# Another order of the weight places, activation sums in the plain units, and a closing step in one piece, in a two-block transformer kernel

## The chip, the core and the metric

The kernel runs on one NeuronCore of a Trainium2 chip. Times are device microseconds (us) of one execution of the whole program. Engines are named as the profile names them: PE does the matmuls, PEld loads their weights, DVE and ACT do the element-wise work, POOL does a little more of it, SP issues the DMAs. The kernel before takes 3473.58 us, the median of 3 runs (3473.26 to 3473.74).

## The reference, cut to what matters

Two transformer blocks over 512 tokens of width 1024, in float32. The first block is a modulated attention-like mixer with one feed-forward part; the second runs twice over: feed-forward, mixer, feed-forward, each followed by a layer norm. So there are five feed-forward parts, and the change lies in them:

```
def swiglu_2(x, w1, w2):
    g, u = jnp.split(x @ w1, 2, axis=-1)
    return (jax.nn.silu(g) * u) @ w2

for l in range(2):
    x = layer_norm(ALPHA * x + 0.5 * swiglu_2(x, ffn_w1[l, 0], ffn_w2[l, 0]), ...)
    x = layer_norm(ALPHA * x + hybrid_mixer_2(x, ...), ...)
    x = layer_norm(ALPHA * x + 0.5 * swiglu_2(x, ffn_w1[l, 1], ffn_w2[l, 1]), ...)
```

The hidden width is 2816, which is 11 column blocks of 256.

## The kernel before, in words

Every float32 operand of a matmul is held as two parts, a rounded value ("hi", cast by ACT) and the rest ("lo", a subtraction on DVE), and a product is three matmuls: hi by hi, hi by lo, lo by hi. In the trace `whi` and `wlo` are the parts of a weight, `xa` is the store of activations XA (its last two slots and some others also serve as weight places), `hl` is the same for the hidden activations, `pj` and `sd` are PSUM tiles.

A feed-forward part (function `ffn`) has three stages.

1. **Plain units.** The first 2 of the 11 hidden blocks are done by ordinary products (`unit`, `mm3`): half of the tokens (H0), then the other half (H1), the last unit whole. Weight pairs go round in a ring of six places: four pairs of slots of XA and two of their own; `plain_mode(e,i)` says at which the ring starts.
2. **Seven-product quads.** The other 9 hidden blocks, and most of the second matrix, are done as `Quad`s: a 2x2 block product with seven instead of eight products, which needs sums of activations (slots S1 to S4 of `Left`; `sums`, `sum4`) and sums of weights (`Quad.sum`). Function `run_quads` writes the order of PE, ACT, DVE and SP by hand, one slot per product: the products of the quads follow each other in a list `seq`; product 7 of a quad comes after product 1 of the next. In a slot come the product itself (`mm`), what closes the product before (`after`), weight sums (`sum`), left-over closing steps (`step`) and the casts of the weight two slots ahead (`cast`, `rest`). Three PSUM banks `sd` are kept: `after(1)` copies product 1 into a bank b (ACT L183), onto which product 2 then adds; product 2 can't start before that copy, and the copy not before the bank's last reader. `seven_mode` opens the stage with 12 small matmuls by zeros (L149), so that later matmuls may add to the banks.
3. **`stage2`**, the rest of the second matrix, and the layer norm.

The quads go in four groups. After each of groups 0, 1 and 2 stand two output quads (`out_quad`, o0 and o1), which read the hidden activations just made; they are called passages here, P1 (after one quad), P2 (after three) and P3 (after two). At a passage the last hidden quad still has to be closed: c12 adds and gates the first half (L258, L260), c21 gates the second (silu L265, L266), then sums for the next products (L110 to L113) and their split (L80 on ACT, L81 on DVE). An output quad adds its four quarters to X (L606, L607): its c22 reads E (a copy of product 4, `t` in the trace, or a bank) and bank b.

The activation sums of XA come in two parts (`e.sums(part,i)`, four tiles i each): part 0 is made in the plain units, part 1 by `extra` in the first slots of the quads; the sums of the two plain hidden blocks (`H.sums`) in slots 4 and 5. In the first feed-forward part (ffn1) all of XA's sums are made before `seven_mode`, and their operands are first remade from hi and lo (L1246). Outside `run_quads` a scheduler orders the instructions on each engine. On each engine all of them run in program order.

Of the kernel before, what the change touches and what calls it, by code (L numbers as in the profile page):

```python
# [88 lines left out]
class Left:  # L89
# [18 lines left out]
    def sum4(s,e,a,b):
        nc=e.nc; t=e.hs.tile([P,4,256],F32,tag="s",name="s",bufs=1)
        nc.vector.tensor_sub(t[:,1,:],b[:,0,:],b[:,1,:])  # L110
        nc.vector.tensor_sub(t[:,0,:],t[:,1,:],a[:,0,:])
        nc.vector.tensor_sub(t[:,2,:],a[:,0,:],b[:,0,:])
        nc.vector.tensor_add(t[:,3,:],t[:,0,:],a[:,1,:])  # L113
        return t
    def sums(s,e,i,a,b,part=None):

        nc=e.nc; n=4 if part is None else 2
        t=e.hs.tile([P,4,256],F32,tag="s",name="s",bufs=1)
        if part!=1:
            nc.vector.tensor_sub(t[:,1,:],b[:,0,:],b[:,1,:])  # L120
            nc.vector.tensor_sub(t[:,0,:],t[:,1,:],a[:,0,:])
        if part!=0: nc.vector.tensor_sub(t[:,n-2,:],a[:,0,:],b[:,0,:])
        if part is None: nc.vector.tensor_add(t[:,3,:],t[:,0,:],a[:,1,:])
        if part==1:
            nc.vector.tensor_sub(t[:,1,:],a[:,1,:],b[:,1,:])
            nc.vector.tensor_sub(t[:,1,:],t[:,1,:],t[:,0,:])
        s.put(e,s.S3 if part==1 else s.S2,n,i,t[:,:n,:])

# [67 lines left out]
def run_quads(e, quads, extra):  # L196
# [18 lines left out]
    with e.tc.manual_schedule(engines={ET.PE,ET.Activation,ET.DVE,ET.SP}):  # L215
        for s in range(min(at),len(seq)+1):
            for q,t in at.get(s,[]):
                if t in (0,5,6): q.load(e,t)
            put=None; keep=None
            if s>0: put=seq[s-1]  # L220
            if 0<=s<len(seq):
                q,j=seq[s]
                for d in q.needs:
                    if j==1: d.all(6)
                    if j==3: d.all(7)
                if j==2 and put==(q,1): q.after(e,1); put=None
                q.mm(e,j)
                if j==7 and s+1<len(seq) and seq[s+1][1]==2: keep=seq[s+1][0]
            if put and not (put[1]==1 and put[0] in done): put[0].after(e,put[1])
            for q,t in at.get(s,[]):  # L230
                if t in (1,2,3,4): q.sum(e,t)
            for q in quads:
                for j in (2,5,6,7):
                    if s>0 and (q,j)!=put: q.step(j)
            if keep in done: keep.after(e,1)
            for f in extra.get(s,[]): f()
            nx=seq[s+2] if 0<=s+2<len(seq) else None
            if nx: nx[0].cast(e,nx[1]); nx[0].rest(e,nx[1])
        for q in quads:
            for j in (2,5,6,7): q.all(j)  # L240
# [10 lines left out]

def gated(e, H, i, hscale, sums):

# [10 lines left out]
    def c21(ps):  # L264
        g=tmp(e); nc.scalar.activation(g,ps,AF.Silu)  # L265
        nc.vector.scalar_tensor_tensor(u.h[:,2:4,:],pair(g),hscale,pair(u.t),op0=ALU.mult,op1=ALU.mult)  # L266
    def c21b(ps):
        if sums: u.s=H.sum4(e,u.h[:,0:2,:],u.h[:,2:4,:])
        H.second(e,i,u.h[:,2:4,:])
    def c21c(ps):  # L270
        if sums: H.put(e,H.S2,4,i,u.s)
    u.c11,u.c12,u.c22,u.c21=[c11],[c12,c12b],[c22],[c21,c21b,c21c]
    return u

GAB=4
GROUPS=((0,3),(3,3),(6,2),(8,3))
PLAIN=2

def ffn(e, w1, w2, acc, hscale, ln):

    nc=e.nc
    with ExitStack() as cf:
# [116 lines left out]
class LN(Norm):  # L399
# [18 lines left out]
    def finish(s,sl):  # L418
# [13 lines left out]
        for i in range(4):  # L432
# [159 lines left out]
def second(e, D, out, layers=2):  # L592

    nc=e.nc
    for l in range(layers):
# [628 lines left out]
class RMS(Norm):  # L1224
# [4 lines left out]
    def finish(s,sl):  # L1229
# [150 lines left out]
```

## Time and profile before

| what | value |
|---|---|
| median of 3 runs | 3473.58 us |
| profiled execution, whole | 3473.03 us |
| its span in the trace | 3471.3 us |
| PE busy | 3272.6 us (94%) |
| DVE busy | 2538.6 us (73%) |
| ACT busy | 1701.5 us (49%) |
| granted TensorE clock, mean | 0.979 |

The stages in the trace (us from the span's start): block 1's mixer to 572, ffn1 from 612 to 1010, ffn2 from 1010 to 1385, a mixer, ffn3 from 1800 to 2235, ffn4 to 2570, a mixer, ffn5 from 3010 to the end. The stage of quads opens at 665, 1042, 1894, 2273 and 3126. The example in the text is mostly ffn3; the others have the same order.

### The profile page before, as it was taken

How to read it: one execution, taken by the hardware profiler on the slowest of the kernel's cores; microseconds unless marked ns; L12 is line 12 of the kernel's file. 1: busy time of each engine (PE TensorE's matmuls, PEld its weight loads, DVE VectorE, ACT ScalarE, POOL GpSimd, SP SyncE). 2: the span in 40 equal slices, each digit the busy share in tenths (PEclk: the TensorE clock that was granted, in tenths of full speed). 3: DMA queues.
4: the chain of work that ended last, by engine and by line, in shares of the span. 5: the costliest groups of instructions: out<-in, count | busy, mean ns of one | idle time of the engine just before them, and what ended most of it. 6: DMA issues, size and time to landing. Idle time of an engine off the chain costs nothing.

```text
span 3471.3 us, 54695 instructions
## 1 busy us (share of the span) xinstructions
PE 3272.6 (94%) x22056; PEld 2997.8 (86%) x22056; DVE 2538.6 (73%) x4061; ACT 1701.5 (49%) x2600; POOL 200.1 (6%) x237
## 2 busy tenths in 40 slices
PE   6979889999998999999999999989999999998998
PEld 3767779999998999878889999989998788898998
DVE  5858877798858988654456898778886634468987
ACT  4544534455544555762224555545556722244554
POOL 3241221000000000110000000000001100000000
PEclk9999999999999999999999999999999999999999
DMA  5221214222322233233331233322333233312231
GB/s 205 67 67 44 78 61 151 71 96 92 106 96 84 92 104 98 91 103 96 97 107 49 86 102 101 110 64 94 94 108 97 92 97 97 110 62 80 96 104 61
DMA packets 103502, 322.09 MB, mean 93 GB/s; under 512 B 11472, under 2 KB 15184, under 8 KB 103248
## 3 DMA queue, kind: packets, MB, share of 16 engines
q1 hardware_dynamic: 102464, 316.04, 28.2%
q8 instruction: 173, 2.83, 0.3%
q0 software_dynamic: 640, 2.10, 0.2%
q14 instruction: 81, 0.66, 0.1%
q10 hardware_dynamic: 144, 0.45, 0.0%
HBM read 316.45 MB, written 2.10 MB: 92 GB/s over the span
## 4 chain that ended last, share of the span: by engine, by line
PE 70%; DVE 16%; ACT 6%; issue 5%; POOL 1%; DMA 1%; ACTq 0%; SPq 0%; DVEq 0%; POOLq 0%
PE sd L134 15%; PE pj L134 12%; PE pj L70 7%; PE pj L71 6%; PE pj L72 6%; PE sd L70 6%; PE sd L71 6%; PE sd L72 6%; DVE wraw L167 2%; DVE wlo L172 1%; DVE cv L913 1%; ACT whi L170 1%; DVE xa L172 1%; DVE X L607 1%; DVE xa L44 1%
## 5 line engine op out<-in xcount | busy, mean ns | idle before, releaser
L43 ACT CAST xa<-wraw 128x1024 fp32r<-128x1024 f32 (+1 forms) x198 | 203.1, 1027 | 377.6 <-issue 172.9
L172 DVE TENSOR_TENSOR wlo<-wraw,whi 128x1024 fp32r<-128x1024 f32 (+2 forms) x310 | 333.5, 1076 | 57.8 <-ACT whi L170 54.0
L44 DVE TENSOR_TENSOR xa<-wraw,xa 128x1024 fp32r<-128x1024 f32 (+1 forms) x188 | 229.3, 1221 | 180.3 <-ACT xa L43 179.7
L70 PE MATMUL pj<-xa 128*128 128x512 f32 (+1 forms) x960 | 336.0, 352 | 3.3 <-ACT xa L80 1.7
L72 PE MATMUL pj<-xa 128*128 128x512 f32 (+1 forms) x960 | 336.3, 351 | 0.2 <-DVE xa L44 0.2
L71 PE MATMUL pj<-xa 128*128 128x512 f32 (+1 forms) x960 | 335.3, 350 | 0.1
L170 ACT CAST whi<-wraw 128x1024 fp32r<-128x1024 f32 (+2 forms) x310 | 286.4, 930 | 48.9 <-DVE wraw L167 24.4
L134 PE MATMUL sd<-xa,whi 128*128 128x256 f32 x2080 | 271.5, 283 | 1.9 <-ACT sd L185 1.9
L134 PEld LDWEIGHTS sd<-xa,whi 128*128 128x128 f32 x2080 | 259.6, 192 | 2.3 <-ACT sd L185 2.3
L70 PE MATMUL sd<-xa 128*128 128x512 f32 (+1 forms) x688 | 233.8, 342 | 2.7 <-ACT xa L80 1.7
L71 PE MATMUL sd<-xa 128*128 128x512 f32 (+1 forms) x688 | 234.8, 342 | 0.0
L72 PE MATMUL sd<-xa 128*128 128x512 f32 (+1 forms) x688 | 234.0, 341 | 0.0
L70 PEld LDWEIGHTS pj<-xa 128*128 128x128 f32 x960 | 184.5, 193 | 23.0 <-ACT X L957 2.0
L134 PE MATMUL pj<-xa,whi 128*128 128x256 f32 x1360 | 183.7, 289 | 20.4 <-ACT sd L183 20.3
L71 PEld LDWEIGHTS pj<-xa 128*128 128x128 f32 x960 | 185.0, 193 | 18.4 <-DVE xa L81 0.5
L72 PEld LDWEIGHTS pj<-xa 128*128 128x128 f32 x960 | 185.0, 193 | 18.0 <-DVE xa L44 0.4
L172 DVE TENSOR_TENSOR xa<-wraw,xa 128x1024 fp32r<-128x1024 f32 (+2 forms) x140 | 152.4, 1088 | 57.5 <-ACT xa L170 19.2
L134 PEld LDWEIGHTS pj<-xa,whi 128*128 128x128 f32 x1360 | 174.4, 198 | 22.7 <-ACT sd L183 22.7
L43 ACT CAST whi<-wraw 128x1024 fp32r<-128x1024 f32 (+1 forms) x90 | 89.4, 1001 | 180.5 <-PE pj L71 95.3
L134 PE MATMUL sd<-xa 128*128 128x256 f32 x1200 | 155.6, 287 | 8.7 <-ACT sd L187 8.7
L167 DVE TENSOR_TENSOR wraw<-wraw 128x1024 f32<-128x1024 f32 (+2 forms) x150 | 160.2, 1076 | 0.2 <-DMA wraw<-in_f_dram 0.2
L134 PEld LDWEIGHTS sd<-xa 128*128 128x128 f32 x1200 | 150.5, 196 | 9.8 <-ACT sd L187 9.8
(559 smaller groups left out, 8166.8 us busy)
## 6 DMA issues: line engine op xcount, KB each, us to landing
wraw<-in_f_dram SPq DMA_DIRECT2D x176, 512.0 KB, 4.1
wraw<-in_win_dram SPq DMA_DIRECT2D x144, 512.0 KB, 3.5
wraw<-in_f_dram SPq DMA_DIRECT2D x96, 384.0 KB, 3.2
wraw<-in_ff_dram SPq DMA_DIRECT2D x44, 512.0 KB, 4.0
raw<-in_ada_dram SPq DMA_DIRECT2D x48, 256.0 KB, 2.6
wraw<-in_ff_dram SPq DMA_DIRECT2D x24, 384.0 KB, 3.2
wraw<-in_ada_dram SPq DMA_DIRECT2D x16, 512.0 KB, 4.1
wraw<-in_f_dram SPq DMA_DIRECT2D x32, 256.0 KB, 2.8
```

The costliest lines, as they stand in the source:

```text
L43: nc.scalar.copy(hi[:,:n],raw[:,:n])
L44: (nc.gpsimd if e.wi%e.gp==0 else nc.vector).tensor_sub(lo[:,:n],raw[:,:n],hi[:,:n].bitcast(F32))
L70: nc.tensor.matmul(o,lhsT=hi[:,c],rhs=ah,start=start and k==k0,stop=False)
L71: nc.tensor.matmul(o,lhsT=hi[:,c],rhs=al,start=False,stop=False)
L72: nc.tensor.matmul(o,lhsT=lo[:,c],rhs=ah,start=False,stop=stop and k==nk-1)
L134: nc.tensor.matmul(ps[:,p*256:p*256+256],lhsT=w[:,j:j+128],rhs=A.t[:,c,k,l,:],start=first,stop=last,skip_group_check=True)
L167: n=s.n; e.nc.vector.tensor_add(o[:,:n],x[:,:n],y[:,:n])
L170: s.w[j]=hilo_tile(e); e.nc.scalar.copy(s.w[j][0][:,:s.n],s.raw(j)[:,:s.n])
L172: hi,lo=s.w[j]; n=s.n; e.nc.vector.tensor_sub(lo[:,:n],s.raw(j)[:,:n],hi[:,:n].bitcast(F32))
L607: else: nc.vector.tensor_tensor(x,x,ps,op=ALU.add if sgn>0 else ALU.subtract)
L913: nc.vector.scalar_tensor_tensor(a[:,o0:o0+n],ci[:,o0+i:o0+i+n],sc(i),a[:,o0:o0+n],op0=ALU.mult,op1=ALU.add)
```

## The change

Five edits:

- The weight ring starts at place 4 (before 0) in the plain units of a feed-forward part and of a mixer, at place 2 (before 4) in `stage2`, and at 1 (before 0) in the stage of quads.
- `seven_mode` clears each bank by one 128x512 matmul by zeros, in place of four 128x128 ones.
- All sums of XA, part 1 and then part 0, and the sums of the first plain hidden block, are made in the plain units (`hsums`, `e.sums`), in tiles of two instead of four; only those of the second plain hidden block are left in the quads, in slot 2.
- At the last hidden quad of a group all of c21 (gate, sums, their split) is issued in one piece (`at_once`). In slots where product 6 or 7 of that quad is closed, the weight sums and casts of the slot come before that closing (`late`).
- An output quad's c22 reads bank b first and then E.

The part on POOL gets no work that it didn't have: `v` is DVE everywhere.

```
     def sums(s,e,i,a,b,part,v=None,last=None):
         t=e.hs.tile([P,2,256],F32,tag="s",name="s",bufs=2)
...
+    def puts(s,e,i,part,t): s.put(e,s.S3 if part else s.S2,2,i,t)
...
-    e.fixed=[e.spare]; e.wide=False; e.wi=0
+    e.fixed=[e.spare]; e.wide=False; e.wi=1
     r=e.XA.t[:,0,0,:,:].rearrange("p l t -> p (l t)")
-    for t in e.sd:
-        for c in range(4): e.nc.tensor.matmul(t[:,c*128:c*128+128],lhsT=e.zero,rhs=e.zero,start=c==0,stop=True,skip_group_check=True)
+    for t in e.sd: e.nc.tensor.matmul(t,lhsT=e.zero,rhs=r,start=True,stop=True)
...
+            nx=seq[s+2] if 0<=s+2<len(seq) else None
+            late=put and put[1] in (6,7) and any(put[0] is q.needs[-1] for q in quads if q.needs)
+            def weights():
+                for q,t in at.get(s,[]):
+                    if t in (1,2,3,4): q.sum(e,t)
+                if nx and late: nx[0].cast(e,nx[1]); nx[0].rest(e,nx[1])
+            if late: weights()
             if put and not (put[1]==1 and put[0] in done): put[0].after(e,put[1])
-            for q,t in at.get(s,[]):
-                if t in (1,2,3,4): q.sum(e,t)
+            if not late: weights()
...
     def c21b(ps):
-        if sums: u.s=H.sum4(e,u.h[:,0:2,:],u.h[:,2:4,:])
+        if sums: u.p0=part(0); u.p1=part(1)
+        if last: H.puts(e,i,0,u.p0)
         H.second(e,i,u.h[:,2:4,:])
+        if last: H.puts(e,i,1,u.p1)
     def c21c(ps):
-        if sums: H.put(e,H.S2,4,i,u.s)
+        if sums and not last: H.puts(e,i,0,u.p0); H.puts(e,i,1,u.p1)
+    if last:
+        def at_once(ps): c21(ps); c21b(ps)
+        u.c21=[at_once]
...
-        plain_mode(e,0)
+        plain_mode(e,4)
...
+        def hsums(q):
+            a,b=hs[q][:,0:2,:],hs[q][:,2:4,:]; t=None
+            for p in (0,1): t=H.sums(e,q,a,b,p,None,t); H.puts(e,q,p,t)
...
-        for i in range(4): e.sums(0,i)
+        for q in range(PLAIN-1): hsums(q)
+        for p in (1,0):
+            for i in range(4): e.sums(p,i)
...
-                x={} if e.early else {0:[lambda: e.sums(1,0)],1:[lambda: e.sums(1,1)],2:[lambda: e.sums(1,2),lambda: e.sums(1,3)]}
-                for i,q in enumerate(range(PLAIN)): x[4+i]=[lambda q=q: H.sums(e,q,hs[q][:,0:2,:],hs[q][:,2:4,:])]
+                x={2: [lambda: hsums(PLAIN-1)]}
...
-    u.c22=[lambda ps,E: into(m+2,H1,E,1,True),lambda ps,E: into(m+2,H1,ps,-1,False)]
+    u.c22=[lambda ps,E: into(m+2,H1,ps,-1,True),lambda ps,E: into(m+2,H1,E,1,False)]
...
-    plain_mode(e,4)
+    plain_mode(e,2)
```

The line numbers shift; those used in the text are, before and after: prod's matmul L134 and L129, the zero matmul L149 and L143, copy of product 1 into b L183 and L177, cast of a weight L170 and L164, its rest L172 and L166, weight sums L167 and L161, c12 L258/L260 and L257/L259, c21 L265/L266 and L264/L265, sums L110 to L113 and L113/L114/L116/L120, sums of XA's part 1 L122/L125/L126 and L116/L118/L119, X L606/L607 and L615/L616.

**Where the quads of ffn3 open**, ACT, from the gate of the last plain unit (L294, after L300) to the first copy of a product 1 into its bank `sd_5190`. `xa<-s` is the cast of a sum of XA, `hl<-h` that of a hidden block. Before:

```order
L294 ACTIVATE t<-pj 128x512
L170 CAST xa<-wraw 128x1024
L170 CAST whi<-wraw 128x1024
L80 CAST hl<-h 128x2x256
L80 CAST hl<-h 128x256
L80 CAST xa<-s 128x2x256
L170 CAST whi<-wraw 128x1024
L183 COPY sd_5190<-pj 128x512
L80 CAST xa<-s 128x2x256
```

After:

```order
L300 ACTIVATE t<-pj 128x512
L80 CAST xa<-s 128x2x256 x2
L164 CAST whi<-wraw 128x1024
L164 CAST xa<-wraw 128x1024
L80 CAST hl<-h 128x2x256
L80 CAST hl<-h 128x256
L177 COPY sd_5190<-pj 128x512
```

The cast of a sum that stood between the hidden block and the copy is gone, and none follows the copy.

**Passage P2 of ffn3**, DVE, from the last quad's c22 (L263, after L262) to the last sum. `sd_5191` holds product 6 with what was added to it, `t_18874` and `t_18912` a weight sum, `hl<-h` and `hl<-s` are the rests of hidden activations and of their sums. Before:

```order
L263 TENSOR_TENSOR t<-t,sd_5190 128x512
L172 TENSOR_TENSOR xa<-wraw,xa 128x768
L258 TENSOR_TENSOR t<-sd_5191,t 128x512
L260 SCALAR_TENSOR_TENSOR h<-g_18804,t 128x512
L167 TENSOR_TENSOR wraw<-wraw 128x768
L172 TENSOR_TENSOR wlo<-wraw,whi 128x768
L81 TENSOR_TENSOR hl<-h,hl 128x2x256
L266 SCALAR_TENSOR_TENSOR h<-t 128x512
L167 TENSOR_TENSOR wraw<-wraw,t_18874 128x768
L172 TENSOR_TENSOR wlo<-wraw,whi 128x768
L110 TENSOR_TENSOR s<-h 128x256
L111 TENSOR_TENSOR s<-s,h 128x256
```

After:

```order
L262 TENSOR_TENSOR t<-t,sd_5190 128x512
L166 TENSOR_TENSOR wlo<-wraw,whi 128x768
L161 TENSOR_TENSOR wraw<-wraw 128x768
L166 TENSOR_TENSOR wlo<-wraw,whi 128x768
L257 TENSOR_TENSOR t<-sd_5191,t 128x512
L259 SCALAR_TENSOR_TENSOR h<-g_18837,t 128x512
L81 TENSOR_TENSOR hl<-h,hl 128x2x256
L161 TENSOR_TENSOR wraw<-wraw,t_18912 128x768
L166 TENSOR_TENSOR xa<-wraw,xa 128x768
L265 SCALAR_TENSOR_TENSOR h<-t 128x512
L113 TENSOR_TENSOR s<-h 128x256
L114 TENSOR_TENSOR s<-s,h 128x256
```

Two instructions on weights (L161, L166) now stand before L257 and L259 instead of behind. On ACT, in the same place, the copy of o0's product 1 (L177) stands behind the silu and the three casts of the piece (`hl<-s`, `hl<-h`, `hl<-s`); before, it stood behind the silu and one cast of a weight, ahead of `hl<-h` and `hl<-s`.

**The same passage, o0's quarters into X**, DVE; `sd_5190` is o0's bank b, which o1's copy of its product 1 takes next. Before:

```order
L607 TENSOR_TENSOR X<-X,t 128x2x256
L167 TENSOR_TENSOR wraw<-wraw,t_19073 128x768
L172 TENSOR_TENSOR wlo<-wraw,whi 128x768
L607 TENSOR_TENSOR X<-X,sd_5191 128x2x256
L607 TENSOR_TENSOR X<-X,sd_5190 128x2x256
```

After:

```order
L616 TENSOR_TENSOR X<-X,sd_5190 128x2x256
L161 TENSOR_TENSOR wraw<-wraw,t_19112 128x768
L166 TENSOR_TENSOR xa<-wraw,xa 128x768
L616 TENSOR_TENSOR X<-X,sd_5191 128x2x256
L616 TENSOR_TENSOR X<-X,t 128x2x256
```

The read of bank b moves ahead of two instructions on weights and of one on X, by one product of a quad.

## Rows read from the trace of the kernel before

**Rows 1.** The page: busy time, share of the span and instructions of each engine.

```profile
PE 3272.6 (94%) x22056; PEld 2997.8 (86%) x22056; DVE 2538.6 (73%) x4061; ACT 1701.5 (49%) x2600; POOL 200.1 (6%) x237
```

**Rows 2.** PE's waits: who waited for whom, us in total, times, longest.

```profile
PE pj L134 <- ACT sd L183: 45.1, 25, 3.6
PE pj L134 <- ACT hl L80: 10.8, 5, 2.2
PE sd L134 <- ACT sd L187: 8.7, 5, 2.2
PE pj L134 <- DVE hl L81: 6.8, 9, 1.3
PE pj L134 <- ACT whi L170: 5.5, 5, 1.7
...
PE sd L134 <- DVE hl L81: 4.4, 5, 0.9
...
PE pj L134 <- DVE xa L172: 3.0, 1, 3.0
...
PE sd L134 <- ACT sd L185: 1.9, 2, 1.7
...
PE sd L134 <- ACT hl L80: 1.7, 5, 0.3
```

**Rows 3.** Half-clock stretches (busy per engine, PEclk, DMA share, GB/s): one of 16, sum.

```profile
1928.23:1935.06 6.83, 5.02 (x22) 4.73 (x23) 6.79 (x12) 3.95 (x7) 0.00 (x0) 0.50 0.01 2
...
sum 71.66, PE 62.73 PEld 61.85 DVE 65.11 ACT 28.64 POOL 0.00; mean PE 3.92 PEld 3.87 DVE 4.07 ACT 1.79 POOL 0.00
```

**Rows 4.** Timeline where ffn3's quads open: start, length, engine, line, idle before.

```profile
1893.41 1.22 DVE L172 TENSOR_TENSOR xa<-wraw,xa 128x1024 fp32r<-128x1024 f32 x1 [9.37 <-PE pj L72]
...
1893.83 1.45 PE L149 MATMUL sd<-zero 128*128 128x128 f32 x12
...
1899.66 0.62 ACT L80 CAST xa<-s 128x512 fp32r<-128x512 f32 x1 [3.47 <-DVE s L126]
...
1901.13 0.58 ACT L183 COPY sd<-pj 128x512 f32<-128x512 f32 x1
...
1901.76 3.79 PE L134 MATMUL pj<-xa,whi 128*128 128x256 f32 x16 [3.56 <-ACT sd L183]
1902.40 0.42 DVE L122 TENSOR_TENSOR s<-X 128x256 f32<-128x256 f32 x1
1902.73 0.42 DVE L125 TENSOR_TENSOR s<-X 128x256 f32<-128x256 f32 x1
```

**Rows 5.** The waits on ACT: its copy into a bank, for the bank's reader.

```profile
ACT sd L183 <- DVE X L607: 69.2, 24, 4.1
```

**Rows 6.** Timeline of ffn3's passage P2, from c12 to o0's product 2.

```profile
2020.95 0.68 DVE L258 TENSOR_TENSOR t<-sd,t 128x512 f32<-128x512 f32 x1
2021.67 0.69 DVE L260 SCALAR_TENSOR_TENSOR h<-g,t 128x512 f32<-128x512 f32 x1
2022.28 0.95 DVE L167 TENSOR_TENSOR wraw<-wraw 128x768 f32<-128x768 f32 x1
...
2022.39 0.62 ACT L80 CAST hl<-h 128x512 fp32r<-128x512 f32 x1 [1.79 <-DVE h L260]
...
2023.36 1.24 PE L134 MATMUL pj<-hl,xa 128*128 128x256 f32 x9
...
2028.09 1.60 PE L134 MATMUL pj<-hl,whi 128*128 128x256 f32 x12
```

**Rows 7.** Timeline of ffn1 before its quads: remade operands on DVE, zeros on PE.

```profile
650.11 1.89 DVE L1246 TENSOR_TENSOR t<-xa 128x512 f32<-128x512 f32 x3
...
665.28 1.45 PE L149 MATMUL sd<-zero 128*128 128x128 f32 x12
```

**Rows 8.** PE alone in two stretches: the norm ffn3 to ffn4, block 1's last chain.

```profile
2222.23:2234.00 11.77, 11.15 (x88) 1.00 0.37 116
565.18:576.30 11.12, 10.72 (x90) 1.00 0.42 133
```

More of the change, by code (lines that the diff above doesn't have):

```diff
@@ L107, in second, with sums @@
         else: s.put(e,s.A22,1,i,b[:,1:2,:])
[L108 to L113, printed above, removed]
-        return t
[L115 to L127, printed above, removed]
+    def sums(s,e,i,a,b,part,v=None,last=None):
+        v=v or e.nc.vector
+        t=e.hs.tile([P,2,256],F32,tag="s",name="s",bufs=2)
+        if part==0:
+            v.tensor_sub(t[:,1,:],b[:,0,:],b[:,1,:])
+            v.tensor_sub(t[:,0,:],t[:,1,:],a[:,0,:])
+        else:
+            v.tensor_sub(t[:,0,:],a[:,0,:],b[:,0,:])
+            if last is None:
+                v.tensor_sub(t[:,1,:],a[:,1,:],b[:,1,:])
+                v.tensor_sub(t[:,1,:],t[:,1,:],t[:,0,:])
+            else: v.tensor_add(t[:,1,:],last[:,0,:],a[:,1,:])
+        return t
+    def puts(s,e,i,part,t): s.put(e,s.S3 if part else s.S2,2,i,t)
 def prod(e, ps, w, A, c, nk, start):
@@ L236, in run_quads @@
             for f in extra.get(s,[]): f()
-            nx=seq[s+2] if 0<=s+2<len(seq) else None
-            if nx: nx[0].cast(e,nx[1]); nx[0].rest(e,nx[1])
+            if nx and not late: nx[0].cast(e,nx[1]); nx[0].rest(e,nx[1])
         for q in quads:
@@ L250, in into_left, with gated @@
         if sums: H.sums(e,i,h[:,0:2,:],h[:,2:4,:])
-def gated(e, H, i, hscale, sums):
+def gated(e, H, i, hscale, sums, last):
     nc=e.nc; u=Use()
@@ L266, in c21, with part @@
         nc.vector.scalar_tensor_tensor(u.h[:,2:4,:],pair(g),hscale,pair(u.t),op0=ALU.mult,op1=ALU.mult)
+    v=nc.vector
+    def part(p): u.s=H.sums(e,i,u.h[:,0:2,:],u.h[:,2:4,:],p,v,p and u.s); return u.s
     def c21b(ps):
-        if sums: u.s=H.sum4(e,u.h[:,0:2,:],u.h[:,2:4,:])
+        if sums: u.p0=part(0); u.p1=part(1)
+        if last: H.puts(e,i,0,u.p0)
         H.second(e,i,u.h[:,2:4,:])
+        if last: H.puts(e,i,1,u.p1)
     def c21c(ps):
-        if sums: H.put(e,H.S2,4,i,u.s)
+        if sums and not last: H.puts(e,i,0,u.p0); H.puts(e,i,1,u.p1)
     u.c11,u.c12,u.c22,u.c21=[c11],[c12,c12b],[c22],[c21,c21b,c21c]
+    if last:
+        def at_once(ps): c21(ps); c21b(ps)
+        u.c21=[at_once]
     return u
@@ L306, in ffn @@
             for half in (0,1): into_left(e,H,j//2,hs[j//2],half,False)
-        if e.early:
-            for i in range(4): e.sums(1,i)
         seven_mode(e); Q=[]
@@ L311, in ffn @@
             last=g==len(GROUPS)-1
-            G=[Quad(e.XA,w1[j],4,gated(e,HP if last else H,j-j0,hscale,not last)) for j in range(max(j0,PLAIN),j0+n)]; Q+=G
+            G=[Quad(e.XA,w1[j],4,gated(e,HP if last else H,j-j0,hscale,not last,not last and j==j0+n-1)) for j in range(max(j0,PLAIN),j0+n)]; Q+=G
             if not last: Q+=[out_quad(e,H,w2[g][i],n,4*i,lambda m,sl,ps,sgn,new,g=g: acc(g,m,2,sl,pair(ps),sgn,new),() if i else G) for i in range(2)]
             else:
-                x={} if e.early else {0:[lambda: e.sums(1,0)],1:[lambda: e.sums(1,1)],2:[lambda: e.sums(1,2),lambda: e.sums(1,3)]}
-                for i,q in enumerate(range(PLAIN)): x[4+i]=[lambda q=q: H.sums(e,q,hs[q][:,0:2,:],hs[q][:,2:4,:])]
+                x={2: [lambda: hsums(PLAIN-1)]}
                 run_quads(e,Q,x)
@@ L439, in finish @@
             if s.out is None: s.to_left(sl,i,X[:,2*i:2*i+2,sl])
-        if sl is H1: e.sums=lambda part,i: e.XA.sums(e,i,X[:,2*i:2*i+2,H0],X[:,2*i:2*i+2,H1],part)
+        if sl is H1: e.sums=lambda part,i: e.XA.puts(e,i,part,e.XA.sums(e,i,X[:,2*i:2*i+2,H0],X[:,2*i:2*i+2,H1],part))
 def proj_units(units, first):
@@ L460, in mixer_in @@
 def mixer_in(e, mx, w_in, w_rg, w_oc, w_or, w_o, C, ln):
-    nc=e.nc; plain_mode(e,0)
+    nc=e.nc; plain_mode(e,4)
     uh=mx.tile([P,8,512],F32R,name="uh"); ul=mx.tile([P,8,512],F32R,name="ul"); U=Flat(uh,ul)
@@ L605, in acc @@
             x=e.X[:,m:m+2,sl] if n==2 else e.X[:,m,sl]
-            if g==0 and new: nc.vector.scalar_tensor_tensor(x,x,ALPHA,ps,op0=ALU.mult,op1=ALU.add)
-            else: nc.vector.tensor_tensor(x,x,ps,op=ALU.add if sgn>0 else ALU.subtract)
+            op=ALU.add if sgn>0 else ALU.subtract
+            if g==0 and new: nc.vector.scalar_tensor_tensor(x,x,ALPHA,ps,op0=ALU.mult,op1=op)
+            else: nc.vector.tensor_tensor(x,x,ps,op=op)
         def mk(i,o=None,r=1.0): return LN(e,C["ln_g"][:,8*i:8*i+8],C["ln_b"][:,8*i:8*i+8],1e-5,o,r)
@@ L1247, in sums @@
         def sums(part,i):
-            if s.b is None: e.XA.sums(e,i,X[:,2*i:2*i+2,H0],X[:,2*i:2*i+2,H1],part)
-            else: e.XA.sums(e,i,again(i,0),again(i,2),part)
-        if sl is H1: e.sums=sums; e.early=s.b is not None
+            a,b=[X[:,2*i:2*i+2,h] for h in (H0,H1)] if s.b is None else (again(i,0),again(i,2))
+            e.XA.puts(e,i,part,e.XA.sums(e,i,a,b,part))
+        if sl is H1: e.sums=sums
 def ada_piece(e,D,at,part,k,tag,raw):
```

## The prediction

> **What bounds the kernel now.** I read the page first, then PE's waits, the timeline around each kind of stop, and the granted clock by stretches. PE is busy for 94% of the span, DVE for 73% [rows 1]; so time can come only from PE's stops, from its clock, or from PE's work. PE's work hardly changes here. The stops that the quads of the five feed-forward parts make are nine lines of PE's waits: 45.1 + 10.8 + 8.7 + 6.8 + 5.5 + 4.4 + 3.0 + 1.9 + 1.7 = 87.9 us [rows 2]. And 16 stretches of 71.66 us in sum ran at half the clock (1.2 of 2.4 GHz), each at or behind a stop, which costs 71.66 / 2 = 35.8 us [rows 3]. More than about 124 us is not to be had.
>
> By place, the 87.9 us are of four kinds.
> - *Opening.* In ffn3 product 2 waits 3.56 us for the copy of product 1 into its bank; the copy stands on ACT behind the cast of a sum of XA, which had ACT idle for 3.47 us before it, for DVE [rows 4]. In all five parts this is 14.6 of the 45.1 us, and the 3.0 and 1.9 us: 19.5.
> - *Product 7 of the first quad*, behind the hidden sums in slots 4 and 5: the 8.7 us, one stop in each part.
> - *Passages.* P1 has 10.8 + 5.5 and five of the nine waits of the 6.8; P3 has the 4.4 and 1.7. Together 29.2 us with the 0.8 of P2, nearly all in P1.
> - *Bank b of an output quad.* Five stops in each part but one: o1's product 2 at P1, P2, P3 and the next quad's product 2 wait for a copy that itself waits for the last reader of the bank, L607 [rows 5]. That is 45.1 − 14.6 = 30.5 us.
>
> **The change, part by part.**
>
> *Sums of XA and of the first hidden block in the plain units.* In ffn2 to ffn5 nothing but the two casts of the hidden block stands ahead of the first copy on ACT. Left is the bare exchange of product 1, copy, product 2: the copy took 0.58 us and product 2 followed 0.63 us after its start [rows 4]; with PE's end ahead of it I take 0.95 us, between 0.63 and the 3.56 of before. Four times: 3.8 us. The sums must fit on DVE: one of part 1 is three subtractions at a step of 0.34 us, the dependent one 0.45, and a rest of about 0.6: 1.75 us, four times 7.0; the hidden sums are four and two rests, 2.8. Those 9.8 us stand against a hole of 9.37 us ahead of DVE's last weight rest before the quads [rows 4]; the first quad's own weight rest comes before the last four sums on DVE in these parts, so I count no stop. In ffn1 it comes behind all of them, and there the operands are remade first: from 650.1 us on DVE has 16 such additions at 0.6 us (1.89 for three, [rows 7]), 9.7 us, sums of 4 x (1.4 + 1.75) = 12.6, hidden ones 2.8, and some 4 of gates and rests: to 679 us. PE wants that rest at 665.28 + 0.7 + 16 x 0.12 = 668 [rows 7]: a stop of 11, with the copy 11.6 us. Its bounds are the 5.1 of before (nothing gets later) and 15. Opening: 3.8 + 11.6 = 15.4, from 19.5.
>
> *Only one set of hidden sums, in slot 2.* Its casts stand two slots ahead of the copy that product 7 waits for. 8.7 goes to 0; what is late next is the copy itself, 0.6 us in each part at the most.
>
> *c22 reads bank b first.* The bank comes free one product earlier, 1.45 to 2.9 us; the stops at o1 were at most 3.6 and mostly 0.8 to 2 long. I leave 0.3 in each part, 1.5 from 30.5. Hidden by PE's product; if DVE is a whole product late, 10 us come back.
>
> *The piece at passages.* At P1 the hidden sums that blocked ACT are gone, and o0's product 1 finds its data. But the copy that o0's product 2 waits for stands behind the whole piece on ACT, with only two products 1 to cover it. At P2, DVE has two weight instructions more ahead of L257, each 0.95 us long and 0.87 from start to start: L257 moves from 2020.95 to 2022.7, h is ready 0.72 + 0.69 later, its cast (0.62) ends at 2024.75, against PE's 2023.36 [rows 6]: a stop of 1.4. Then the products 1 of o0 and o1 last 2 x 2.2 us, to 2029.2. Meanwhile DVE has 0.6 (rest), 2 x 0.87 (weights), 0.6 (gate) and four sums of about 0.4, to 2029.3, ACT's casts follow with about 1.2, then the copy's 0.63: 2031.0. That stop is 1.8; P2 costs 3.2, from 0.16. At P3 the weights are narrower, but so are the covering products: 3.2 again. At P1 only the second stop remains, 1.75. Sum 8.15, in five parts 40.8, from 29.2. Bounds: the bare exchange of 0.95 at each passage (14) and P1 as it was, (10.8 + 5.5 + 6.8) / 5 = 4.6 [rows 2], at each (69). I take the worked-out value.
>
> *Zeros.* Twelve matmuls of 128 columns take 1.45 us [rows 4]; three of 512 take 3 x 0.23 if 256 columns take 0.12, as the quads' do (9 in 1.24, [rows 6]). 5 x 0.75 = 3.8 saved, at least 0, since twelve to three can't be slower.
>
> *The ring's start and the order outside the quads.* These shift what the scheduler lays under the norms. Between ffn3 and ffn4, 88 PE instructions lay under the norm's chain, 63 of them matmuls of the next units [rows 8]; now about 17: 46 x 0.12 = 5.6 us lost. In block 1's last chain about 60 of 90 [rows 8] are gone from under it; all of them would be 7.2, some of it is cover that wasn't needed; I take 4. These 9.6 have bounds of 0 and 13.
>
> *Clock.* Stops that stay are followed by half clock as the rows had it: each P2 and P3 one stretch of 3.4 us (10 x 1.7 = 17 lost), ffn1's opening 6.8 (3.4), the norm and the end 4.5: 25, from 35.8. Bounds: 8 (no passage is followed) and 51 (every passage by 6.83 us, as P1 of ffn3 was, [rows 3]).
>
> A stop as P2's, in two parts of under 2 us, is the open case. P1 of ffn3 had three, of 2.2 us at the most [rows 2], and 6.83 us at half clock [rows 3]. The Trainium skill (TensorE: Matmul & The Clock Gate, section "HAM oscillation — how this bites in real kernels") says that one long idle gap between bursts makes the next burst start throttled; by that alone P2 and P3 would be free of it, 17 us less, and the result 3421. Its next section ("A second HAM failure mode: psum-queue depth-cycling") says that frequent short stops at the turn of PSUM banks do it as well; this one the trace bears out, and it speaks against the piece.
>
> *Sum.* Stops: 15.4 + 0 + 1.5 + 40.8 = 57.7, from 87.9: −30.2. Zeros −3.8, cover +9.6, clock −10.8. Together −35.2: 3473.03 − 35.2 = 3437.8 for a profiled execution; the median of the runs shown lies 0.55 above it: 3438.
>
> **The rivals.**
> - *The passages are free.* If DVE is done earlier than I lay it (it was 73% busy overall), only the exchange is left: 40.8 falls to 14 and the clock's loss to 8. −27 − 17: 3394. For it: every waiting instruction moved was moved ahead of need. Against: the copy stands behind three casts, whatever DVE does.
> - *The passages cost as much as P1 did.* 15 x 4.6 = 69 in place of 40.8, and 9 more of clock: 3438 + 28 + 9 = 3475, no change. For it: P1's stops came from the very work that is now in one piece at all three. Against: it had double sums there.
> - *Slower: DVE is behind when the quads open.* The 9.8 us of sums go into a hole of 9.37, and they also wait for the XA slots that the weights leave, which the new ring decides. If in ffn2 to ffn5 the first weight rest is late as in ffn1, each has 10 us more of stop and 3.4 of clock: 4 x 13.4 = 54, 3492. It decides from 9 us a part on. Against: the rest stands ahead of the last sums.
>
> **How the numbers follow.** The forecast has 0.62, with its own range 3420 to 3456 (clock −17 or +9, passages ±10); free passages 0.14, dear passages 0.11, DVE behind 0.13. No change is within 0.2%, 7 us. Faster by more has 0.62 + 0.14 + 0.02 = 0.78, slower by more 0.11 + 0.03 = 0.14, the rest 0.08. The range goes from 3402 to 3478: it leaves out half of the free passages, most of DVE behind and a part of the dear ones.
>
> **What would show it.** Right: PE's wait for the copy into b at one place per passage (15 times, 1.7 to 2.4 us) and nearly none at o1; no wait for product 7's copy; one stop of 10 us or more in ffn1's opening and about 1 us in the others; ffn3 to ffn4 longer by 5 us; half clock near 50 us in the feed-forward parts. Wrong: stops of 5 us at the openings of ffn2 to ffn5 (the third rival), waits at P2 and P3 over 4 us or under 1 us.

## The result, and the profile after

The changed kernel takes 3426.51 us, the median of 4 runs (3419.30 to 3430.60), against 3473.42 before (4 runs): a ratio of 0.9861, interval 0.9846 to 0.9876. It is faster by 47 us; 35 were forecast, and the time lies inside the range given. The profiled execution is the longest of the four, 3430.60 us (3473.03 before).

The page's first part after, to set beside [rows 1]:

```profile
PE 3263.1 (95%) x22011; PEld 2989.2 (87%) x22011; DVE 2539.7 (74%) x4101; ACT 1709.2 (50%) x2640; POOL 199.3 (6%) x237
```

The work is the same but for 45 zero matmuls fewer. PE's idle time in the span fell from 3471.3 − 3272.6 = 198.7 us to 3428.8 − 3263.1 = 165.7, its busy time by 9.5: stops and clock have moved. PE's waits after, those of the quads (who waited for whom, us in total, times, longest), answer to [rows 2]:

```profile
PE pj L129 <- ACT sd L177: 33.1, 22, 2.2
...
PE pj L129 <- DVE wlo L166: 8.8, 5, 6.0
...
PE pj L129 <- DVE hl L81: 5.1, 15, 0.3
...
PE pj L129 <- ACT hl L80: 3.2, 10, 1.0
...
PE sd L143 <- ACT t L300: 2.7, 1, 2.7
...
PE pj L129 <- DVE xa L166: 0.5, 1, 0.5
```

They come to 53.4 us, from 87.9. The wait for product 7's copy (8.7) is gone. The copy L177 is waited for 22 times: at five openings, at 15 passages before o0's product 2 (1.7 to 2.2 us each), and twice in ffn3 for a bank b (0.90 before o1's product 2 at P3, 0.82 before the next quad's). DVE's reads of X no longer hold that copy: [rows 5] with its 69.2 us has no counterpart among ACT's longest waits. Of the waits for L166 only the 6.0 belongs to ffn1's opening. The other four (1.14 in ffn1, 0.57 or 0.58 in ffn2, ffn4 and ffn5) and the 0.5 are new: they stand in and behind P3, four of them in the product 2 that waited for bank b before. There the rest of a weight on DVE now comes last.

P2 of ffn3, the timeline after (start, length, engine, line, idle before), answers to [rows 6]:

```profile
1999.20 0.68 DVE L257 TENSOR_TENSOR t<-sd,t 128x512 f32<-128x512 f32 x1
...
1999.92 0.69 DVE L259 SCALAR_TENSOR_TENSOR h<-g,t 128x512 f32<-128x512 f32 x1
1999.96 1.12 PE L129 MATMUL pj<-hl,whi 128*128 128x256 f32 x8
2000.64 0.62 ACT L80 CAST hl<-h 128x512 fp32r<-128x512 f32 x1 [3.44 <-DVE h L259]
...
2001.32 0.38 PE L129 MATMUL pj<-hl,whi 128*128 128x256 f32 x1 [0.23 <-ACT hl L80]
...
2002.04 0.61 PE L129 MATMUL pj<-hl,whi 128*128 128x256 f32 x3 [0.34 <-DVE hl L81]
...
2005.28 0.62 ACT L80 CAST hl<-s 128x512 fp32r<-128x512 f32 x1 [2.79 <-DVE s L114]
...
2006.11 0.62 ACT L80 CAST hl<-s 128x512 fp32r<-128x512 f32 x1
...
2006.63 0.58 ACT L177 COPY sd<-pj 128x512 f32<-128x512 f32 x1
...
2007.26 3.92 PE L129 MATMUL pj<-hl,xa 128*128 128x256 f32 x18 [1.73 <-ACT sd L177]
```

Read it from below: o0's product 2 starts 0.63 us after the start of its copy, which ran behind the casts of the piece, the first of which had ACT idle for 2.79 us, for DVE's sums. All five P2 look like this (in ffn4 the first stop is 0.98 in place of 0.23), P1 too.

ffn1's opening after, PE alone:

```profile
673.83 0.62 PE L143 MATMUL sd<-xa,zero 128*128 128x512 f32 x2
...
679.04 0.49 PE L143 MATMUL sd<-xa,zero 128*128 128x512 f32 x1 [2.67 <-ACT t L300]
...
685.51 2.08 PE L129 MATMUL pj<-xa,wlo 128*128 128x256 f32 x8 [5.98 <-DVE wlo L166]
...
688.34 2.08 PE L129 MATMUL pj<-xa,whi 128*128 128x256 f32 x8 [0.74 <-ACT sd L177]
```

9.4 us, where it was 5.1. The stretches at half clock in ffn1 to ffn5 (columns as in [rows 3]), the first, one at a passage, the one in the norm behind ffn3, and the sum of 8:

```profile
679.63:693.28 13.65, 7.02 (x31) 6.73 (x32) 11.38 (x18) 4.66 (x7) 0.00 (x0) 0.50 0.09 29
...
2007.41:2010.82 3.41, 3.41 (x17) 3.41 (x18) 1.98 (x3) 1.94 (x3) 0.00 (x0) 0.50 0.00 0
...
2205.38:2215.62 10.24, 9.66 (x43) 9.39 (x44) 5.88 (x11) 3.44 (x6) 0.00 (x0) 0.50 0.49 148
...
sum 44.35, PE 37.14 PEld 36.58 DVE 30.29 ACT 15.91 POOL 0.00; mean PE 4.64 PEld 4.57 DVE 3.79 ACT 1.99 POOL 0.00
```

44.35 us against 71.66, so 13.7 us regained, if half of a stretch's length counts as lost. And two losses outside the quads, PE in the stretch from the norm's first matmuls by `ident` (L364, after L372) behind ffn3 to ffn4's first product, and from 500 us to ffn1's first product, after:

```profile
2192.75:2259.52 66.77, 62.60 (x438) 0.92 0.18 58
499.96:674.29 174.33, 165.78 (x1183) 0.97 0.34 110
```

and before:

```profile
2213.35:2274.23 60.88, 59.59 (x447) 1.00 0.26 89
495.30:666.57 171.27, 165.51 (x1194) 0.98 0.35 112
```

5.9 and 3.1 us lost. The 10.24 us at half clock of the norm lie inside the first stretch, so 5.1 of its 5.9 us stand in the 44.35 already, and 0.8 is left. Between the two executions 4.7 us more were also spent before 500 us, where the order of PE did not change, and 3 us less in the second mixer, where two half-clock stretches are missing. The 4.7 us are the spread of executions: PE's 2400th matmul starts between 483.8 and 490.2 us in the 14 kernels traced here, and latest in this trace.

### The profile page after: what moved, and what is told of

Same layout as the page of the kernel before. It is cut to its first block, busy times and chain, and to the rows that moved or that the text cites. A ratio compares the mean times of both kernels' runs of the same rounds, so it can differ in the third digit from the quotient of the medians.

```text
span 3428.8 us, 54643 instructions
## 1 busy us (share of the span) xinstructions
PE 3263.1 (95%) x22011; PEld 2989.2 (87%) x22011; DVE 2539.7 (74%) x4101; ACT 1709.2 (50%) x2640; POOL 199.3 (6%) x237
## 5 line engine op out<-in xcount | busy, mean ns | idle before, releaser
L166 DVE TENSOR_TENSOR wlo<-wraw,whi 128x1024 fp32r<-128x1024 f32 (+2 forms) x295 | 316.3, 1074 | 48.3 <-ACT whi L164 46.1
L70 PE MATMUL pj<-xa 128*128 128x512 f32 (+1 forms) x968 | 343.1, 355 | 1.4 <-ACT X L966 1.4
L72 PE MATMUL pj<-xa 128*128 128x512 f32 (+1 forms) x968 | 341.9, 354 | 0.0
L71 PE MATMUL pj<-xa 128*128 128x512 f32 (+1 forms) x968 | 341.3, 353 | 0.0
L164 ACT CAST whi<-wraw 128x1024 fp32r<-128x1024 f32 (+2 forms) x295 | 272.3, 926 | 61.5 <-DVE wraw L161 26.2
L129 PE MATMUL sd<-xa,whi 128*128 128x256 f32 x1760 | 229.1, 283 | 0.0
L129 PEld LDWEIGHTS sd<-xa,whi 128*128 128x128 f32 x1760 | 219.1, 192 | 0.0
L129 PE MATMUL sd<-xa 128*128 128x256 f32 x1680 | 213.0, 283 | 0.0
L129 PEld LDWEIGHTS sd<-xa 128*128 128x128 f32 x1680 | 206.6, 192 | 0.0
L71 PE MATMUL sd<-xa 128*128 128x512 f32 (+1 forms) x600 | 204.7, 341 | 0.0
L70 PE MATMUL sd<-xa 128*128 128x512 f32 (+1 forms) x600 | 203.8, 341 | 0.9 <-DVE X L1230 0.9
L129 PE MATMUL pj<-xa,whi 128*128 128x256 f32 x1520 | 200.0, 285 | 4.2 <-ACT sd L177 4.2
L72 PE MATMUL sd<-xa 128*128 128x512 f32 (+1 forms) x600 | 203.8, 340 | 0.0
L129 PEld LDWEIGHTS pj<-xa,whi 128*128 128x128 f32 x1520 | 190.9, 193 | 5.9 <-ACT sd L177 5.5
L44 DVE TENSOR_TENSOR wlo<-wraw,whi 128x1024 fp32r<-128x1024 f32 (+1 forms) x88 | 109.1, 1241 | 97.6 <-ACT whi L43 97.1
L166 DVE TENSOR_TENSOR xa<-wraw,xa 128x1024 fp32r<-128x1024 f32 (+2 forms) x155 | 169.5, 1094 | 16.0 <-ACT xa L164 14.4
```

Of the source, the lines that this page charges most:

```text
L44: (nc.gpsimd if e.wi%e.gp==0 else nc.vector).tensor_sub(lo[:,:n],raw[:,:n],hi[:,:n].bitcast(F32))
L70: nc.tensor.matmul(o,lhsT=hi[:,c],rhs=ah,start=start and k==k0,stop=False)
L71: nc.tensor.matmul(o,lhsT=hi[:,c],rhs=al,start=False,stop=False)
L72: nc.tensor.matmul(o,lhsT=lo[:,c],rhs=ah,start=False,stop=stop and k==nk-1)
L129: nc.tensor.matmul(ps[:,p*256:p*256+256],lhsT=w[:,j:j+128],rhs=A.t[:,c,k,l,:],start=first,stop=last,skip_group_check=True)
L164: s.w[j]=hilo_tile(e); e.nc.scalar.copy(s.w[j][0][:,:s.n],s.raw(j)[:,:s.n])
```

## The experiments

All were run beside the kernel before on the same chip; medians in us, with their runs. Experiments on the changed kernel are read against its 3426.5 (3419.3 to 3430.6). It was not run again beside them; the kernel before had medians of 3471.3 to 3474.4 there, so differences of less than about 3 us mean nothing.

**The bank read undone** (on the changed kernel):

```
-    u.c22=[lambda ps,E: into(m+2,H1,ps,-1,True),lambda ps,E: into(m+2,H1,E,1,False)]
+    u.c22=[lambda ps,E: into(m+2,H1,E,1,True),lambda ps,E: into(m+2,H1,ps,-1,False)]
```

> The changed kernel with one thing undone: the output quads' c22 reads E first and bank b second, as before. Theory (the bank that comes free a product earlier was the largest single saving): the stops at o1's product 2 and at the next quad's product 2 come back, about 30 us of PE waiting for the copy L177 at these places, and 3 to 9 us of half clock behind them: 3455 to 3466 us. Rival (o1 was relieved because the sums left the slots around it, c22's order is worth little): 3424 to 3432 us, and no new stop at o1.

3464.6 (3457.1 to 3469.4): 38 us lost by one swapped line. PE's waits:

```profile
PE pj L129 <- ACT sd L177: 65.1, 40, 4.4
```

18 more waits for the copy than the changed kernel has, 32 us more, as the theory had it. Against that the small waits for L166 are gone; only ffn1's 6.0 is left:

```profile
PE pj L129 <- DVE wlo L166: 6.0, 1, 6.0
```

ffn3's worst, before o1's product 2 at P3, shows the chain whole:

```profile
2106.09 1.28 DVE L616 TENSOR_TENSOR X<-X,sd 128x512 f32<-128x512 f32 x2
...
2107.45 0.57 ACT L177 COPY sd<-pj 128x512 f32<-128x512 f32 x1 [2.01 <-DVE X L616]
...
2108.08 1.10 PE L129 MATMUL pj<-hl,whi 128*128 128x256 f32 x7 [2.79 <-ACT sd L177]
```

**The bank read alone** (the same two lines exchanged in the kernel before, with the sign taken into `acc`):

> The kernel before with one edit alone: the output quads' c22 reads bank b first, then E. Theory (the copy of o1's product 1 and of the next quad's waits only for this read): PE's waits for the copy L183 fall by about 30 us, to 15, and some of the half clock goes with them: 3432 to 3443 us. Rival (its worth comes only together with the sums that left the slots, so that DVE is in time): PE's waits for the copy stay above 30 us, 3455 to 3468 us.

3443.4 (3443.0 to 3444.4), 31 us faster than the 3474.4 beside it. PE's waits:

```profile
PE pj L134 <- ACT sd L183: 16.7, 7, 3.6
...
PE pj L134 <- DVE wlo L172: 3.3, 5, 1.1
```

From 45.1 us in 25 waits to 16.7 in 7: it needs none of the other edits. The 3.3 us for weights' rests (L172) are new here too, at the same places as in the changed kernel, so 25 us of stops are gone in all.

**The sums back in the quads** (on the changed kernel; shortened):

```
-        for q in range(PLAIN-1): hsums(q)
-        for p in (1,0):
-            for i in range(4): e.sums(p,i)
+        for i in range(4): e.sums(0,i)
...
-                x={2: [lambda: hsums(PLAIN-1)]}
+                x={} if e.early else {0:[lambda: e.sums(1,0)],1:[lambda: e.sums(1,1)],2:[lambda: e.sums(1,2),lambda: e.sums(1,3)]}
+                for q in range(PLAIN): x[4+q]=[lambda q=q: hsums(q)]
```

> The changed kernel with the sums where they were: XA's part 1 in the first slots of the quads (in ffn1 behind the units), the hidden sums in slots 4 and 5; still in tiles of two. Theory (the sums on ACT and DVE held the opening, product 7 of the first quad and P1): the opening stops of ffn2 to ffn5 rise from 0.9 to 2.7 to 5 us each, product 7 waits 1.7 to 2.2 us five times, P1 costs 4 to 5 in place of 2.3; ffn1's opening falls from 9.4 to 5 us. In sum 28 to 35 us and 5 to 10 of clock: 3460 to 3472 us. Rival (tiles of two and the other edits have made them harmless there): 3424 to 3438 us.

3485.1 (3477.4 to 3487.1): 59 us slower than the changed kernel, more than the 34 to 46 forecast, and slower than the kernel before. PE in ffn3 from product 7 of the first quad to P1:

```profile
1925.85 3.14 PE L129 MATMUL sd<-xa,whi 128*128 128x256 f32 x16 [3.13 <-ACT sd L181]
1931.44 1.21 PE L129 MATMUL pj<-hl,whi 128*128 128x256 f32 x8 [0.96 <-ACT whi L164]
1936.15 1.74 PE L129 MATMUL pj<-hl,whi 128*128 128x256 f32 x4 [3.50 <-ACT hl L80]
```

Product 7 waits 3.13 us (1.68 in the kernel before), and P1 3.50 in one stop; each of the five P1 has such a stop (3.35 to 3.50 us), and 6.83 us at half clock go with it each time. A collision of the sums with the piece and the weights that now go ahead of it would explain it; that was not tested by itself. ffn1's opening didn't fall to 5 us either: it is one stop of 8.88 for the copy. The direction is the theory's; the size holds stops that neither kernel has.

**The piece in two**:

```
-        def at_once(ps): c21(ps); c21b(ps)
-        u.c21=[at_once]
+        u.c21=[c21,c21b]
```

> The changed kernel with the piece at passages cut in two: the gate (silu, L265) in the slot of o0's product 1, sums and splits in the slot of o1's product 1, so that on ACT the copy of o0's product 1 stands ahead of the three casts. Theory (o0's product 2 waits 1.7 to 2.2 us at each of 15 passages only because the copy stands behind the casts): these stops fall to under 0.3 us each, 28 us in sum; the sums come later, and before o0's product 3 up to 0.8 us may be lost each time; with 3 to 8 us of clock 3395 to 3412 us. Rival (the sums are what is short, the stop only moves from product 2 to product 3): 3423 to 3432 us, and PE waits for L80 or L81 of the sums instead.

3390.1 (3384.3 to 3391.1), 36 us faster than the changed kernel, and better than its theory's range. PE's waits for the copy fall from 33.1 to

```profile
PE pj L129 <- ACT sd L177: 4.9, 7, 0.9
...
PE sd L129 <- ACT whi L164: 3.7, 5, 0.8
```

and the stop doesn't move to product 3, but for 0.74 to 0.76 us at each P3. No stretch of the quads behind the openings is at half clock.

**Weights not ahead of the closing**:

```
-            late=put and put[1] in (6,7) and any(put[0] is q.needs[-1] for q in quads if q.needs)
+            late=False
```

> The changed kernel without the rule that in the slots where product 6 or 7 of the last hidden quad is closed the weight sums and casts come first. Theory (the rule puts two weight instructions ahead of c12 at P2 and P3 and so costs the 0.6 us that o0's product 1 waits there, but the weights of the output quads are needed just after): the stops for c12 go at P2 and P3, 10 times 0.3 to 0.6, and at most as much comes back as waits for weights: 3420 to 3432 us, no difference that can be told. Rival (the rule is what holds the weights of o0 and o1 in time): waits for L164 or L166 at each passage, 15 times 1 to 1.7 us, and 3440 to 3455 us.

3398.9 (3398.0 to 3400.0): both expectations fail, it is 28 us faster. P2 of ffn3:

```profile
1988.55 0.57 ACT L177 COPY sd<-pj 128x512 f32<-128x512 f32 x1
...
1989.18 2.41 PE L129 MATMUL pj<-hl,xa 128*128 128x256 f32 x18 [0.72 <-ACT sd L177]
```

0.72 us in place of 0.23 + 0.34 + 1.73. P1 and P2 of all five parts have 0.72; at P3 one stop of 1.89 us stays. Two weight instructions on DVE (0.95 us each) had pushed the whole closing back, the gate, the sums, the casts and the copy behind them, not only c12; and the weights, when they come later, are still in time: no wait for L164 or L166 appears at P1 or P2. PE's waits for the copy:

```profile
PE pj L129 <- ACT sd L177: 21.7, 22, 1.9
```

**Both of these**:

> Both of the last two edits at once: the piece in two, and weights not ahead of the closing. Theory (the two costs lie in different products and add): as the kernel with two pieces, less 0 to 5 us: 3392 to 3412 us. Rival (DVE is the bound at the passages, whatever the order): within 4 us of the changed kernel, 3422 to 3431 us.

3381.0 (3380.7 to 3383.0), faster than either expectation, 45 us below the changed kernel. Alone the edits bring 36 and 28: they share the stop at o0's product 2, which either shortens.

**The closing in three steps as before, and no weights ahead of it** (`last` passed as False, `late=False`):

> The changed kernel with this part of the change fully undone: at passages the closing goes in three steps as in the kernel before (gate; sums and the split of the second half; split of the sums), and weights are not put ahead of it. Theory (the piece and the weights ahead of it cost 45 us in the changed kernel, and the sums have a slot to spare even in three steps at P1 and P2): stops at o0's product 2 gone, 1 to 1.3 us at P3 before o0's product 3 as before: 3378 to 3390 us. Rival (in three steps the sums come too late for o0's product 3, which is what the piece was for): 1 to 2 us of waiting for L80 or L81 at each of 15 passages, 3395 to 3415 us.

3383.8 (3381.1 to 3384.1), 43 us below the changed kernel, as its theory had it: this part of the change costs that much in the changed kernel. At P1 and P2 of ffn3 no stop is left, at P3 0.67 before o0's product 3, for L81.

**stage2's ring at place 4 as before**:

```
-    plain_mode(e,2)
+    plain_mode(e,4)
```

> The changed kernel with stage2's ring starting at place 4 as before. Theory (the start of the ring decides which weights are ready under the norms' chains): the 60 matmuls come back under block 1's last chain and the stretch from 500 us to ffn1's first product is 2 to 5 us shorter, and about half of the cover comes back between ffn3 and ffn4, 2 to 4 us: 3418 to 3424 us. Rival (the ring of the plain units sets the cover, not this one): both stretches within 1 us of the changed kernel, 3424 to 3430 us.

3414.4 (3408.1 to 3417.9), 12 us faster, more than either expectation. The two stretches outside the quads:

```profile
2184.99:2243.71 58.72, 56.45 (x420) 1.00 0.25 84
493.61:663.97 170.36, 164.64 (x1184) 0.98 0.34 112
```

8.0 and 4.0 us shorter than in the changed kernel, and the first at full clock. The norm's stop behind ffn3 (3.61 us) is gone with its half clock. PE's waits for DVE's lnQ, in the changed kernel and here:

```profile
PE ps L367 <- DVE lnQ L399: 5.7, 4, 3.6
...
PE ps L367 <- DVE lnQ L399: 1.5, 2, 1.3
```

**ffn1's remade operands used twice** (for each i both parts of the sums at once; 8 additions fewer):

> The changed kernel with ffn1's remade operands used for both parts of the sums at once: 8 additions on DVE in place of 16, nothing else. Theory (ffn1's opening stop of 9.4 us is DVE's queue ahead of the first weight rest): 8 x 0.6 = 4.8 us less queue, the stop falls to 4 to 5.5 us, and the half clock behind it from 13.65 to 7 to 10 us: 5 to 8 us less, 3418 to 3422 us. Rival (the stop belongs to the last unit's silu, which sits behind the casts of sums on ACT): the stop stays above 8 us, 3424 to 3429 us.

3416.5 (3413.8 to 3418.7), 10 us faster. ffn1's opening:

```profile
679.33 2.08 PE L129 MATMUL pj<-xa,wlo 128*128 128x256 f32 x8 [3.49 <-DVE wlo L166]
682.63 1.65 PE L129 MATMUL pj<-xa,whi 128*128 128x256 f32 x6 [1.22 <-ACT sd L177]
```

4.7 us, and the wait for the last unit's silu is gone too: it sat behind casts that waited for the same DVE queue. Of the 10 us, 4.7 are the stop and 1.7 its half clock (10.24 us in place of 13.65). The profiled execution also has half clock behind two passages in place of six, though the passages' stops are the same.

**The plain units' ring at place 0** (`plain_mode(e,0)` in `ffn`). With it the last two weight pairs of the plain units go into two of the slots in which the sums of XA have just been put, so that the quads multiply by something else; the instructions are the same.

> The changed kernel with the ring of the plain units of the feed-forward parts starting at place 0 as before. Theory (the start at place 4 has the weights leave the slots of the sums S3 and S2 early enough for the sums to be made before the quads): the sums wait on DVE for PE's last read of these slots, the first weight rest behind them, and ffn2 to ffn5 open with stops of 3 to 6 us in place of 0.7 to 0.9; about 3 us come back as cover between ffn3 and ffn4: 3432 to 3450 us. Rival (the start matters only for the cover under the norms, where the old one had more): 3414 to 3424 us, openings as in the changed kernel.

3472.0 (3466.1 to 3481.0): all of the gain gone. But the theory's place was wrong, since the openings have no longer stops than before. They stand earlier, in the plain units:

```profile
1891.70 0.80 PE L70 MATMUL pj<-xa 128*128 128x512 f32 x1 [5.15 <-ACT xa L43]
```

The last unit's weights wait for their slot until the sums in it are through, and in each part the plain units' stops for such weights come to 3.6 to 12.6 us. The start at 4 gives that unit the ring's own two places: it is a condition of sums made in the plain units, not a gain of its own. PE's waits for lnQ are 1.5 us here as well, and no half clock follows the norm: the stop behind ffn3 takes both new ring starts, that of the plain units and that of `stage2`, and putting back either removes it.

**Twelve zero matmuls as before**:

> The changed kernel with the banks cleared by twelve matmuls of 128 columns as before. Theory (twelve take 1.45 us, three of 512 columns 0.7): 5 x 0.75 = 3.8 us more where nothing else waits, that is in ffn2 to ffn5, where the weights' rests have that much time: 3426 to 3431 us, inside the spread of the changed kernel's own runs. Rival (the time is taken back, since product 1 then finds its weight ready and the copy is the wait anyhow): within 1 us.

3432.1 (3428.4 to 3433.3). The medians differ by 5.6, but the runs of the two kernels overlap; that it is worth the 3.8 us forecast is neither shown nor excluded.

**The four edits that gained, together**:

> The changed kernel with the four edits that made it faster one by one: the piece in two, weights not ahead of the closing, stage2's ring at place 4, ffn1's remade operands used twice. Theory (they lie in different stretches: passages, the norms' chains, ffn1's opening): 45 us for the two at the passages, 12 and 10 for the others, 3426 - 67 = 3359, from 3355 to 3366 us. Rival (a part of each was half clock, which the others take too): 3366 to 3376 us.

3368.2 (3365.7 to 3371.3), ratio to before 0.9693 (0.9680 to 0.9705): the fastest version, 58 us below the changed kernel, not the 67 of the sum. PE's waits in its quads:

```profile
PE pj L129 <- ACT sd L177: 7.4, 8, 1.8
...
PE pj L129 <- DVE wlo L166: 6.3, 5, 3.5
PE sd L129 <- ACT whi L164: 5.3, 5, 1.1
```

That fits the rival, by which a part of each gain was half clock that the others take too. The profiled executions show such a part: the half clock behind four passages that the shared operands were without (4 x 1.7 = 6.8 us) also goes with the passages' stops. How much of the missing 9 us this is in the medians is not shown.

Three details of the change were not undone by themselves: the sums' tiles of two, the ring's start in the mixers, and its start at 1 in the stage of quads.

## Why the prediction was right, and where its sizes were off

- **Bank b.** Forecast 30.5 to 1.5 us of stops. The waits for the copy fell to 1.7 (0.90 and 0.82, both in ffn3), but 3.3 us of waits for weights' rests on DVE took their place in and behind P3 (0.48 and 1.14 in ffn1, 0.57 or 0.58 in three more parts): 5.1 in all. The forecast didn't ask what would be last once the bank was free. Undoing the edit costs 38 us, doing it alone brings 31: shown both ways, with the clock behind it. (The bank had four stops in each part, 20 in all, none longer than 2.95 us; the forecast's five and 3.6 are slips that its sum doesn't use.)
- **Sums in the plain units.** Product 7's 8.7 us to 0: measured 0. Openings of ffn2 to ffn5 0.95 each: measured 0.93 and three times 0.66. The third rival (DVE behind in these openings) did not come: the 9.8 us of sums found their hole. Its remark that the new ring decides was right, as the plain units' ring at place 0 showed.
- **ffn1's opening.** Forecast 11.6, measured 9.4. 5.98 of it is the wait for the first weight rest that was forecast; 2.67 stand earlier, at the third zero matmul, for the last unit's silu, which the forecast didn't have. 8 additions less took 4.7 of the whole.
- **Passages.** Mechanism right, size 40.8 against 36.4 (P1 2.3, P2 2.3, P3 2.5 in most parts, against 1.75, 3.2, 3.2). L257 moved back by 1.64 us against PE's product 7, 1.75 was worked out. The step that failed is the stop of 1.4 at o0's product 1: its first 8 matmuls read the two older hidden blocks, 0.96 us of cover that I left out, and 0.57 was lost. The second stop was 1.73, forecast 1.8. What the working didn't see is that the same two instructions made most of the second stop as well: without them P2 costs 0.72 in all.
- **The rival of free passages** priced them at 3394. The changed kernel isn't it, but the kernels with the closing in two or three steps and no weights ahead of it are, at 3381 and 3384: the price was near, and the condition is the order, not DVE's speed.
- **Cover.** Forecast 5.6 and 4, measured 5.9 and 3.1. The first agrees by luck: 5.1 of the 5.9 are half clock behind a stop of 3.61 us for lnQ, and 0.8 is left for the cover that was meant. The forecast had allowed 4.5 of clock for the norm and the end together, so the same loss lay in its clock term as well. That the rings' starts decide was right: with `stage2`'s put back both stretches are shorter than in the kernel before.
- **Clock.** Forecast 25 us lost, measured 44.35 / 2 = 22.2. Six of the 15 passages of this execution were followed by a half-clock stretch, three P2 and three P3; I had counted ten. Of the two sections of the Trainium skill (TensorE: Matmul & The Clock Gate) weighed there, "HAM oscillation — how this bites in real kernels" alone would have given none, since no gap of a passage is long by itself; "A second HAM failure mode: psum-queue depth-cycling" is borne out in six of 15. Neither says which.

Between the two profiled executions 42.4 us were gained, 35.2 forecast. Stops fell by 34.5 (87.9 to 53.4) against 30.2: openings (12.3 against 15.4) and passages came out cheaper than forecast, the bank's places dearer, and these errors partly cancel. The clock gave 13.7 against 10.8. The two stretches outside the quads cost 9.0 against 9.6, 5.1 of which the clock's account holds already. The medians differ by 47 because this profile (3430.6) is the longest of four.

By undoing parts, the change reads: bank b 38 and sums 59 gained, zeros perhaps 6, against 43 lost by the closing in one piece with weights ahead of it and 12 by `stage2`'s ring: 48. The parts are not independent, and the 59 holds stops that neither kernel has, so this is a reading and not a proof. Three measured steps lead from one kernel to the other without them: the bank read alone, 3474.4 to 3443.4 (31 gained); then the sums in tiles of two, the zeros and the rings together, to the 3383.8 of the closing in three steps (60 gained; the kernel before lay at 3474.4 and 3474.3 beside these two); then the closing in one piece with weights ahead of it, to 3426.5 (43 lost). The 47 us are a large gain and a large loss.

## What to carry to other kernels

A copy that frees a bank for the next product should stand ahead of everything on its engine that isn't needed sooner; issuing a closing step in one piece puts the copy behind the slowest of its inputs. When instructions are moved ahead on a busy engine, count the delay for all that follows in the chain, not only for the next reader, and ask whether what was moved had slack where it stood. Read a shared buffer first when another engine waits for it, and the private one second: here one swapped line was worth 31 to 38 us. When a wait goes, look for what comes last behind it: here 3.3 us of the 30.5 came back as waits for weights' rests.

## What was not expected of the hardware

The granted clock did not follow the length of a stop. In the changed kernel's trace the 15 stops for o0's copy last 1.72 to 2.16 us; behind six of them the clock fell to half for 3.41 us, behind nine it stayed at full, and stops of 1.73 us stand on both sides. Three other kernels have the same 15 stops: with `stage2`'s ring at place 4 half clock follows at seven, with the twelve zero matmuls at six, with ffn1's shared operands at two. Without weights ahead of the closing it follows four of the five stops of 1.89 us at P3. What decides is not shown.

The four runs of the changed kernel, with the same instructions, go with their clock: 3419.3 us at a mean granted clock of 0.984, 3426.0 at 0.982, 3427.0 at 0.981, 3430.6 at 0.980. These stops are not the whole of the spread, though: the kernel with the piece in two has, in its profiled execution, no half clock in the quads behind the openings, and its runs still spread over 6.8 us.

Shortening the stops at P1 and P2 from 1.7 to 0.72 us, without weights ahead of the closing, was worth more than the stops: PE's idle time from 540 us to its last matmul fell by 20 us (76.5 to 56.6), the run time by 28. Two half-clock stretches fewer behind passages (3.4 us) are a part of the rest; the remainder was not traced.
